# Modulation sums by whole rows, tied in program order, and moved later

## The chip, the cores and the metric

The kernel runs on one core of a Trainium2 chip. The metric is the device time in microseconds. Engines named below: PE (TensorE, matrix multiply), DVE (VectorE), ACT (ScalarE), POOL (GpSimd) and SP (SyncE, whose queue issues most transfers).

## The reference

512 latent tokens and 256 context tokens of width 1024 pass through two blocks of two layers each, in float32. Every layer begins with a modulated norm, whose shift, scale and gate are a vector times a matrix:

```python
shift_x, scale_x, gate_x = jnp.split(jax.nn.silu(c) @ w_mod + b_mod, 3, axis=-1)
hx = rms_norm(xs, norm_g) * (1 + scale_x[:, None]) + shift_x[:, None]
...                                     # block 1: conv, GLA and attention branches
xs = xs + gate_x[:, None] * merge(px, ya_x, yb_x, yc_x)
```

In block 1 the context has its own modulation from `c_ctx` and the same matrix; its second layer updates the latent alone. In block 2 `silu(c_2) @ w_ada` gives shift, scale and gate of each layer; the layers mix with mLSTM heads and retention heads.

## The kernel before

Activations lie as [128 partitions, 8 x tokens]. Every projection is three matmuls of split halves (`mm3`, line 315). A weight pack of 512 KB is loaded on the SP queue (`raw`, line 268), its high part is copied by ACT (line 283), its low part subtracted by DVE (line 284); two raw and two split packs exist at a time.

**Modulation.** Layer 0 of block 1 gets its shift and scale at the start, by matmuls. All other 80 groups of 128 outputs ("rows", one tile of [128, 1024] weights each) are multiplied and summed on DVE: `mod_gen` loads a half row of 512 columns (line 404, SP queue, tag `mw`, four buffers, three loads ahead) and runs a multiply-sum instruction per half row and vector (line 415; the profile shows it as a custom instruction and a read of the accumulator). A first half starts from the bias, a second half from the first's result. Rows for layer 0's gates and for layer 1's shift and scale are summed with two vectors (`c`, `c_ctx`). `conditions` loads the vectors and applies silu, half a row at a time (lines 382 to 389).

**Order of the work.** The program is traced once, layer by layer; generators are woven by hand (`_weave`, `_lifted`). Each `proj_gen` and each piece of `proj_n` ends in a `tick`, which adds `bg_rate` to an account and for every whole unit on it advances the list `K.bg` by a step: a half row, or a vector of `conditions`. `K.bg` is filled ahead of each layer's attention stage: in layer 0 with the conditions, `gate0` and `mod1` at 1.4 a tick, in layer 1 with the third condition, `mod2` and `mod3` at 1.2. `drain` runs what is left of a named list: `gate0` and the next layer's list before the layer's last projection, `mod3` before the end of block 2's first layer.

After tracing, a planner puts each engine's instructions in order: by its own times, of what is ready it takes what was traced first, so an instruction that is ready early can pass others that wait. `_lifted` makes it prefer a generator by 200 places. `tc.keep_in_program_order(ins)` ties an instruction behind the one traced before it on its engine; what comes later isn't tied by it.

**Stages.** Layer 0: start to 65 us; conv taps on DVE (line 806) beside projections; conv norm (lines 820 to 868); four GLA heads (lines 930 to 1025; a reciprocal square root, `rsqrt`, lines 300 to 306, in each head's two segments) woven with the first merge; attention (`kv_in`, `grp_in`, `heads`) woven with `gated` and the second merge; then the gated attention output, the third merge (`merge(ab_, "w_attn_out", 2, done=fin)`) and the output projection. Layer 1 is the same with 512 tokens in the outputs. Block 2 runs from some 1630 us.

Of the kernel before, what the change touches and what calls it, by code (L numbers as in the profile page):

```python
# [9 lines left out]
F32 = mybir.dt.float32  # L10
F32R = mybir.dt.float32r
BF16 = mybir.dt.bfloat16
U8 = mybir.dt.uint8
I32 = mybir.dt.int32
AF = mybir.ActivationFunctionType
ALU = mybir.AluOpType
# [3 lines left out]
P = 128  # L20
D = 1024
# [236 lines left out]
class _K:  # L258
# [33 lines left out]
    def rsqrt(self, x, tag=""):  # L292

        V = self.nc.vector
        n = x.shape[1]
# [81 lines left out]

    def conditions(self, first, n):

        S = self.nc.scalar  # L380
        self.cond = self.cst.tile([P, 2, D], F32, tag="cond", name="cond")
        S.dma_start(out=self.cond[:, :n, :], in_=self.a["cond"][:, first:first + n, :])
        for i in range(n):
            for o in range(0, D, 512):
                c = self.cond[:, i, o:o + 512]
                t = self.mp.tile([P, 512], F32, tag="mw", name="mt")
                S.activation(t, c, AF.Tanh, scale=0.5)
                S.activation(c, c, AF.Copy, scale=0.5)
                self.nc.vector.scalar_tensor_tensor(out=c, in0=t, scalar=1.0, in1=c, op0=ALU.add, op1=ALU.mult)
            yield True  # L390

    def mod_gen(self, idx, todo):


        V = self.nc.vector
        todo = [(j, vecs, o) for j, vecs in todo for o in (0, 1)]
        out, bias = self.mods[idx], self.bmod[idx]
        ws, part = [], {}

        def load(n):  # L400
            if n < len(todo):
                j, _, o = todo[n]
                w = self.mp.tile([P, 512], F32, tag="mw", name="mw")
                self.nc.sync.dma_start(out=w, in_=self.a["modw"][idx, j, :, 512 * o:512 * o + 512])
                ws.append(w)
        for n in range(3):
            load(n)
        for n, (j, vecs, o) in enumerate(todo):
            load(n + 3)
            w = ws.pop(0)  # L410
            for v, b in vecs:
                if o == 0:
                    part[b] = self.mp.tile([P, 1], F32, tag=f"pt{b}", name="pt", bufs=2)
                junk = self.mp.tile([P, 512], BF16, name="junk", bufs=1)
                V.tensor_tensor_reduce(out=junk, in0=w, in1=self.cond[:, v, 512 * o:512 * o + 512], scale=1.0,  # L415
                                       scalar=part[b] if o else bias[:, j:j + 1], op0=ALU.mult, op1=ALU.add,
                                       accum_out=out[:, j, b:b + 1] if o else part[b])
            yield True


# [39 lines left out]
    def hidden(self, x, rstd, i, b, s, e, k, t3):  # L460

        V, S = self.nc.vector, self.nc.scalar
        t = t3()[:, :e - s]
        sh = self.mods[i][:, k, b:b + 1]
        V.scalar_tensor_tensor(out=t, in0=x[:, k, s:e], scalar=self.gsc[:, k, b:b + 1], in1=rstd, op0=ALU.mult,
                               op1=ALU.mult)
        S.activation(self.hh[:, k, s:e], t, AF.Identity, bias=sh)
        V.scalar_tensor_tensor(out=self.hl[:, k, s:e], in0=t, scalar=sh, in1=self.hh[:, k, s:e].bitcast(F32),  # L468
# [104 lines left out]
def _first_block(K, ctx, resp):  # L573
    tc, nc, a = K.tc, K.nc, K.a
    V, S, G, T = nc.vector, nc.scalar, nc.gpsimd, nc.tensor
    ident, ones, eps = K.ident, K.ones, K.eps
# [7 lines left out]
    def layer(l, res, t3p, ctx2, pend):  # L584
# [57 lines left out]
        mod = K.mods[l]  # L642
        first = None
        if l == 0:
            with tc.tile_pool(name="m0", bufs=16) as m0, tc.tile_pool(name="m0ps", bufs=1, space=PSUM) as mq:
# [38 lines left out]
                ws = [mod_in(p_, 0) for p_ in (0, 1)]  # L684
# [361 lines left out]
            _weave(gla, merge(cb, "w_conv_out", 0, True), n_gla - n0, 24 if need else 16)  # L1046


        if l == 0:
            K.bg = [("c", K.conditions(0, 2)),  # L1050
                    ("gate0", K.mod_gen(0, [(j, ((0, 0), (1, 1))) for j in range(16, 24)])),
                    ("mod1", K.mod_gen(1, [(j, ((0, 0), (1, 1)) if j < 16 else ((0, 0),)) for j in range(24)]))]
            K.bg_rate = 1.4
        else:
            K.bg = [("c", K.conditions(2, 1))]
            K.bg += [(f"mod{i}", K.mod_gen(i, [(j, ((0, 0),)) for j in range(24)])) for i in (2, 3)]
            K.bg_rate = 1.2


        with tc.tile_pool(name="att", bufs=1) as ap, tc.tile_pool(name="attps", bufs=1, space=PSUM) as pa:  # L1060
# [185 lines left out]
            def heads(g, ao):  # L1246
                prev = None
                qTs = [head_in(g, 0)]
                for i in range(4):
# [14 lines left out]
            _weave(_chain(heads(0, ao), grp_in(1), heads(1, ao)), _lifted(tc, merge(gb_, "w_gla_out", 1), 200),  # L1264
                   *((114, 32) if need else (72, 16)))

        ab_ = []
        for _ in gated(ao, C_AG, "bag", 0.5, ab_, U, A):
            pass
# [33 lines left out]
        with tc.tile_pool(name="nps", bufs=4, space=PSUM) as nps:  # L1303
            if not need:
                K.new_h()

            K.drain("gate0", f"mod{l + 1}")

            def norm_a():
                if need:  # L1310
                    K.new_h()
                K.gains(l + 1)
                return K.norm_gen(new, accA, l + 1, 0, *A, t3, lambda: nps.tile([P, 512], F32, name="nps"))
            K.out_norm(K.out_gen("w_out", l, 0, mhl, A, B, evac, not need), norm_a)
# [12 lines left out]
def _second_block(K, ctx, res, pend):  # L1327
    tc, nc, a = K.tc, K.nc, K.a
    V, S, G, T = nc.vector, nc.scalar, nc.gpsimd, nc.tensor
# [49 lines left out]
    def last(acc, s, e):  # L1379
        r = []  # L1380
        yield from K.rstd_gen(acc, pb, r)
        for k in range(KT):
# [4 lines left out]
            if k % 2:  # L1387
                yield

    norm_b = pend(tt, pb)  # L1390
    PAIRS = [(i, j) for j in range(4) for i in range(j, 4)]
    PIDX = {p: n for n, p in enumerate(PAIRS)}
# [3 lines left out]
    for l in range(DEPTH):  # L1396
# [8 lines left out]
        mod = K.mods[2 + l].rearrange("p a b -> p (a b)")  # L1405
# [237 lines left out]
        for hd in range(4):  # L1643
            y += mixer("m", hd)
            if l == 0 and hd == 0:
                tables()
        for ob in range(KT):
            evac(ob, *K.proj_t(("w_out_2", l, 0, 8, 128 * ob, 128), y, XS)[0])
        y = []
# [21 lines left out]
def build(tc, a):  # L1671
    nc = tc.nc
    K = _K(tc, a)
    with ExitStack() as ctx:
        cst = K.cst = ctx.enter_context(tc.tile_pool(name="cst", bufs=1))
        K.identr = cst.tile([P, P], F32R, name="identr")
        K.ident = K.identr.bitcast(F32)
        K.ones = cst.tile([P, 8], F32, name="ones")
        nc.gpsimd.memset(K.ones, 1.0)
        K.eps = cst.tile([P, 1], F32, name="eps")  # L1680
        nc.gpsimd.memset(K.eps, EPS)
        K.hpi = cst.tile([P, 1], F32, name="hpi")
        nc.gpsimd.memset(K.hpi, float(np.pi / 2))
        V, S = nc.vector, nc.scalar
        c1_, c2_ = _S1["c"], _S2["c"]
        cv = cst.tile([P, 24], F32, name="cv")
        S.dma_start(out=cv[:, 0:16], in_=a["small1"][0, :, c1_:c1_ + 16])
        S.dma_start(out=cv[:, 16:24], in_=a["small2"][0, :, c2_:c2_ + 8])
        K.bmod = []
        for i, (arr, l, off) in enumerate((("small1", 0, _S1["bmod"]), ("small1", 1, _S1["bmod"]),  # L1690
                                           ("small2", 0, _S2["bada"]), ("small2", 1, _S2["bada"]))):
            t = cst.tile([P, 24], F32, name=f"bmod{i}")
            S.dma_start(out=t, in_=a[arr][l, :, off:off + 24])
            K.bmod.append(t)
        K.ngs = []
        for i, (arr, l, off) in enumerate((("small1", 0, _S1["ng"]), ("small1", 1, _S1["ng"]),
                                           ("small2", 0, _S2["ng"]), ("small2", 1, _S2["ng"]))):
            t = cst.tile([P, 8], F32, name=f"ng{i}")
            S.dma_start(out=t, in_=a[arr][l, :, off:off + 8])
            K.ngs.append(t)  # L1700
        K.mods = [cst.tile([P, 24, 2 if i < 2 else 1], F32, name=f"mod{i}") for i in range(4)]
        ct = cst.tile([P, 24], F32, name="ct")
        S.activation(ct, cv, AF.Tanh, scale=0.5)
        V.tensor_scalar(out=cv, in0=cv, scalar1=0.5, scalar2=None, op0=ALU.mult)
        V.scalar_tensor_tensor(out=ct, in0=ct, scalar=1.0, in1=cv, op0=ALU.add, op1=ALU.mult)
        K.cpad = cst.tile([P, KT, 32], F32, name="cpad")
        nc.gpsimd.memset(K.cpad, 0.0)
        V.tensor_copy(out=K.cpad[:, :, 0:3], in_=ct.rearrange("p (b k) -> p k b", b=3))
        K.selm = cst.tile([P, 3], F32, name="selm")
        S.dma_start(out=K.selm, in_=a["selm"])  # L1710
        K.sp = ctx.enter_context(tc.tile_pool(name="sp", bufs=2))
        K.mp = ctx.enter_context(tc.tile_pool(name="mp", bufs=4))
        K.wr = ctx.enter_context(tc.tile_pool(name="wr", bufs=2))
        K.wh = ctx.enter_context(tc.tile_pool(name="wh", bufs=2))
        K.hp = ctx.enter_context(tc.tile_pool(name="hid", bufs=1))
        eye = K.mp.tile([P, 256], F32, name="accB", bufs=1)
        nc.scalar.dma_start(out=eye[:, :P], in_=a["ident"])
        S.activation(K.identr, eye[:, :P], AF.Copy)
        resp = ctx.enter_context(tc.tile_pool(name="resp", bufs=1))
        with ExitStack() as c1:  # L1720
            x, pend = _first_block(K, c1, resp)
        with ExitStack() as c2:
            _second_block(K, c2, x, pend)
# [20 lines left out]
```

## Time and profile before

| | |
|---|---|
| median of 3 runs | 2816.28 us (2813.78 to 2820.03) |
| profiled execution, its time | 2818.03 us |
| its span | 2816.2 us |
| mean granted PE clock | 0.966 of full speed |
| busy in the span | PE 94%, PEld 81%, DVE 71%, ACT 38%, POOL 1% |
| chain that ended last | PE 79%, DVE 13%, ACT 3%, issue 2%, DMA 2% |
| line 404 (`mw`) transfers | 160 of 256 KB, median 3.1 us to landing |
| line 268 (`wr`) transfers | 308 of 512 KB, 3.6 us; 48 of 256 KB, 2.7 us |

Busy time is what an engine spent in instructions; matmuls are pipelined, so their durations overlap and a busy PE need not be at its peak. The granted clock is the share of full speed that PE was given. The chain is followed back from the last instruction to what released each step. A wait is put down to the event that came last.

### The profile page before, as it was taken

To read this page: it belongs to the slowest core of one execution; us is meant where nothing else is said; L and a number is where in the kernel's file an instruction comes from. 1 tells how busy PE (TensorE), PEld (TensorE's weight loads), DVE (VectorE), ACT (ScalarE), POOL (GpSimd) and SP (SyncE) were. 2 spreads that over 40 slices of the span, in tenths; PEclk is the share of its full clock that TensorE was granted. 3 is DMA by queue.
4 is the path that set the end of the run, shared out by engine and by line. 5 is a ranking of instruction groups with operands and counts; after the bars stand their busy time and mean duration, and the time that the engine had idled before them with its cause. 6 is when DMAs were issued, how large, how long until landed. Compare 5 with 4: busy or idle time off the path is not lost.

```text
span 2816.2 us, 38989 instructions
## 1 busy us (share of the span) xinstructions
PE 2646.8 (94%) x15260; PEld 2290.9 (81%) x15260; DVE 2003.1 (71%) x3912; ACT 1082.4 (38%) x1800; POOL 25.9 (1%) x93
## 2 busy tenths in 40 slices
PE   5897798799999999699999999999999999999998
PEld 4786677788888878577888898888888988888887
DVE  5999988877763489777678477764666687745655
ACT  4243332245552233343456345442333444432332
POOL 0000000000000000000000000000000000000000
PEclk9998898799999999799999999999999999999999
DMA  6221345630111322112211332222232222322322
GB/s 241 77 66 49 113 136 184 201 97 30 42 47 60 109 86 70 34 49 75 74 53 46 98 103 85 83 76 80 81 95 68 83 78 90 90 68 83 93 73 75
DMA packets 89208, 242.26 MB, mean 86 GB/s; under 512 B 11200, under 2 KB 17728, under 8 KB 88768
## 3 DMA queue, kind: packets, MB, share of 16 engines
q1 hardware_dynamic: 83968, 233.38, 27.2%
q10 hardware_dynamic: 5056, 6.39, 0.7%
q8 instruction: 120, 1.97, 0.3%
q14 instruction: 64, 0.52, 0.1%
HBM read 237.64 MB, written 2.10 MB: 85 GB/s over the span
## 4 chain that ended last, share of the span: by engine, by line
PE 79%; DVE 13%; ACT 3%; issue 2%; DMA 2%; DVEq 0%; ACTq 0%
PE pp L315 63%; PE pm L315 5%; PE ov L1236 2%; DVE ca L806 2%; PE sc L1206 2%; PE tr L1226 2%; DVE SP L992 2%; DVE wl L284 1%; DVE junk L415 1%; DMA mw<-modw 1%; ACT wh L283 1%; PE pm L1017 1%; PE pm L621 1%; PE pm L631 1%; PE pm L1013 1%
## 5 line engine op out<-in xcount | busy, mean ns | idle before, releaser
L315 PE MATMUL pp<-hh,wh 128*128 128x512 f32 (+1 forms) x2080 | 774.8, 375 | 21.5 <-ACT wh L283 8.9
L315 PE MATMUL pp<-hh,wl 128*128 128x512 f32 (+1 forms) x2080 | 770.6, 373 | 16.2 <-DVE wl L284 16.2
L315 PE MATMUL pp<-hl,wh 128*128 128x512 f32 (+1 forms) x2080 | 771.0, 372 | 1.5 <-DVE hl L468 1.3
L283 ACT ACTIVATE wh<-wr 128x1024 fp32r<-128x1024 f32 (+1 forms) x316 | 314.1, 995 | 731.4 <-PE pp L315 615.1
L284 DVE TENSOR_TENSOR wl<-wr,wh 128x1024 fp32r<-128x1024 f32 (+1 forms) x316 | 360.2, 1140 | 221.5 <-ACT wh L283 218.7
L315 PEld LDWEIGHTS pp<-hh,wh 128*128 128x128 f32 x2080 | 398.9, 192 | 89.0 <-ACT wh L283 11.1
L315 PEld LDWEIGHTS pp<-hh,wl 128*128 128x128 f32 x2080 | 398.6, 192 | 87.1 <-DVE wl L284 20.8
L315 PEld LDWEIGHTS pp<-hl,wh 128*128 128x128 f32 x2080 | 399.0, 192 | 66.2 <-DVE hl L468 3.4
L806 DVE SCALAR_TENSOR_TENSOR ca<-u,sm,ca 128x783 f32<-128x783 f32 (+1 forms) x240 | 200.8, 886 | 0.4
L315 PE MATMUL pp<-hl,hh 128*128 128x256 f32 x544 | 155.8, 286 | 2.6 <-DVE hl L284 2.5
L315 PE MATMUL pp<-hh 128*128 128x256 f32 x544 | 155.5, 286 | 0.9 <-ACT u L1502 0.9
L315 PE MATMUL pp<-hh,hl 128*128 128x256 f32 x544 | 155.3, 285 | 0.0
L315 PE MATMUL pp<-wl,hh 128*128 128x256 f32 x448 | 128.6, 288 | 1.7 <-DVE wl L284 1.7
L315 PE MATMUL pp<-wh,hh 128*128 128x256 f32 x448 | 126.6, 288 | 3.6 <-ACT tf L736 3.6
L315 PE MATMUL pp<-wh,hl 128*128 128x256 f32 x448 | 127.4, 286 | 0.0
L315 PE MATMUL pp<-bh,wh 128*128 128x512 f32 (+1 forms) x288 | 104.9, 367 | 9.0 <-ACT bh L864 6.6
L315 PEld LDWEIGHTS pp<-hl,hh 128*128 128x128 f32 x544 | 105.7, 194 | 4.1 <-DVE hl L284 3.5
L315 PEld LDWEIGHTS pp<-hh 128*128 128x128 f32 x544 | 105.8, 194 | 3.2 <-ACT u L1502 1.7
L315 PEld LDWEIGHTS pp<-hh,hl 128*128 128x128 f32 x544 | 105.9, 195 | 0.0
L315 PE MATMUL pp<-bh,wl 128*128 128x512 f32 (+1 forms) x288 | 103.3, 360 | 0.7 <-DVE wl L284 0.7
L315 PE MATMUL pp<-bl,wh 128*128 128x512 f32 (+1 forms) x288 | 103.5, 361 | 0.0
L315 PE MATMUL pp<-yh,wh 128*128 128x512 f32 (+1 forms) x256 | 94.5, 369 | 0.0
(372 smaller groups left out, 4930.2 us busy)
## 6 DMA issues: line engine op xcount, KB each, us to landing
wr<-wpack SPq DMA_DIRECT2D x308, 512.0 KB, 3.6
mw<-modw SPq DMA_DIRECT2D x160, 256.0 KB, 3.1
wr<-wpack SPq DMA_DIRECT2D x48, 256.0 KB, 2.7
m<-wpack SPq DMA_DIRECT2D x16, 512.0 KB, 8.9
res<-xT SPq DMA_DIRECT2D x4, 512.0 KB, 5.0
tf<-xT SPq DMA_DIRECT2D x8, 256.0 KB, 2.8
out<-t SPq DMA_DIRECT2D x16, 128.0 KB, 1.8
cond<-cond ACTq DMA_DIRECT2D x1, 1024.0 KB, 8.5
```

Of the source, the lines that this page charges most:

```text
L283: self.nc.scalar.activation(hi, r, AF.Copy)
L284: self.nc.vector.tensor_tensor(out=lo, in0=r, in1=hi.bitcast(F32), op=ALU.subtract)
L315: mm(o, lhsT=lhs[a], rhs=r[b], start=first and p == 0, stop=last and p == 2)
L415: V.tensor_tensor_reduce(out=junk, in0=w, in1=self.cond[:, v, 512 * o:512 * o + 512], scale=1.0, scalar=part[b] if o else bias[:, j:j + 1] ...
L621: T.matmul(p1[:, i:i + 1], lhsT=x[:, o:o + P], rhs=ones[:, 0:1], start=True, stop=True)
L631: T.matmul(p2[:, o:o + P], lhsT=r[:, i:i + 1].to_broadcast([P, P]), rhs=ident, start=True, stop=True)
L806: V.scalar_tensor_tensor(out=ca[:, c, :], in0=x, scalar=w, in1=ca[:, c, :], op0=ALU.mult, op1=ALU.add)
L992: V.scalar_tensor_tensor(out=SP[r, n_, :], in0=SP[r, c_, :], scalar=dec[r, c_:c_ + 1], in1=con[c_][r, :], op0=ALU.mult, op1=ALU.add)
L1013: T.matmul(op[:, p * P:p * P + P], lhsT=gv[:, p0 + p, vh], rhs=asum[:, p * P:p * P + P], start=True, stop=False)
L1206: T.matmul(sc[:, s - k0:e - k0], lhsT=qT[:, t * P:t * P + P], rhs=kT[pi][:, s:e], start=pi == 0, stop=pi == 1)
L1226: T.transpose(tr[:, jj * 256 + q * P:jj * 256 + q * P + P], pr[q][:, (j + jj) * P:(j + jj + 1) * P], ident)
L1236: T.matmul(ov, lhsT=vhl[:, kts[j0 + jj], g].rearrange("p a b -> p (a b)"), rhs=x_[:, jj * 256:jj * 256 + 256], start=j0 + jj + pi == 0, st ...
```

## The change

Whole rows: `mw` tiles hold 1024 columns, in two buffers instead of four, one load ahead instead of three, and one multiply-sum serves a row and vector; the account's unit is a row, and a list's first step is its first load alone. Each multiply-sum, and the Tanh and the last instruction of `conditions`, are tied in program order. The rates and lists are new: 0.3 a tick from the attention stage on, 1.3 from the gated attention output on (under the third merge), 0.5 from block 2 on; layer 0 has the conditions, `gate0` and the 16 rows of layer 1's shift and scale; the other rows are in layer 1's lists, with a drain for `gate2` in block 2.

```diff
     def conditions(self, first, n):
...
-            for o in range(0, D, 512):
...
+            c = self.cond[:, i, :]
+            t = self.mp.tile([P, D], F32, tag="mw", name="mt")
+            pin(S.activation(t, c, AF.Tanh, scale=0.5))
+            S.activation(c, c, AF.Copy, scale=0.5)
+            pin(self.nc.vector.scalar_tensor_tensor(out=c, in0=t, scalar=1.0, in1=c, op0=ALU.add, op1=ALU.mult))
             yield True
     def mod_gen(self, idx, todo):
-        V = self.nc.vector
-        todo = [(j, vecs, o) for j, vecs in todo for o in (0, 1)]
+        V, pin = self.nc.vector, self.tc.keep_in_program_order
...
-                w = self.mp.tile([P, 512], F32, tag="mw", name="mw")
-                self.nc.sync.dma_start(out=w, in_=self.a["modw"][idx, j, :, 512 * o:512 * o + 512])
+                w = self.mp.tile([P, D], F32, tag="mw", name="mw")
+                self.nc.sync.dma_start(out=w, in_=self.a["modw"][idx, todo[n][0]])
                 ws.append(w)
-        for n in range(3):
-            load(n)
-        for n, (j, vecs, o) in enumerate(todo):
-            load(n + 3)
+        load(0)
+        yield True
+        for n, (j, vecs) in enumerate(todo):
+            load(n + 1)
             w = ws.pop(0)
             for v, b in vecs:
...
+                junk = self.mp.tile([P, D], BF16, name="junk", bufs=1)
+                pin(V.tensor_tensor_reduce(out=junk, in0=w, in1=self.cond[:, v, :], scale=1.0,
+                                           scalar=bias[:, j:j + 1], op0=ALU.mult, op1=ALU.add,
+                                           accum_out=out[:, j, b:b + 1]))
             yield True
...
+        c_x, c_ctx = (0, 0), (1, 1)
         if l == 0:
             K.bg = [("c", K.conditions(0, 2)),
-                    ("gate0", K.mod_gen(0, [(j, ((0, 0), (1, 1))) for j in range(16, 24)])),
-                    ("mod1", K.mod_gen(1, [(j, ((0, 0), (1, 1)) if j < 16 else ((0, 0),)) for j in range(24)]))]
-            K.bg_rate = 1.4
+                    ("gate0", K.mod_gen(0, [(j, (c_x, c_ctx)) for j in range(16, 24)])),
+                    ("mod1", K.mod_gen(1, [(j, (c_x, c_ctx)) for j in range(16)]))]
         else:
-            K.bg = [("c", K.conditions(2, 1))]
-            K.bg += [(f"mod{i}", K.mod_gen(i, [(j, ((0, 0),)) for j in range(24)])) for i in (2, 3)]
-            K.bg_rate = 1.2
+            K.bg = [("gate1", K.mod_gen(1, [(j, (c_x,)) for j in range(16, 24)])),
+                    ("c", K.conditions(2, 1)),
+                    ("mod2", K.mod_gen(2, [(j, (c_x,)) for j in range(16)])),
+                    ("gate2", K.mod_gen(2, [(j, (c_x,)) for j in range(16, 24)])),
+                    ("mod3", K.mod_gen(3, [(j, (c_x,)) for j in range(24)]))]
+        K.bg_rate = 0.3
...
+        K.bg_rate = 1.3
         ab_ = []
...
-            K.drain("gate0", f"mod{l + 1}")
+            K.drain("gate0", "mod1", "gate1", "mod2")
...
+    K.bg_rate = 0.5
     norm_b = pend(tt, pb)
...
+        K.drain("gate2")
         for ob in range(KT):
             evac(ob, *K.proj_t(("w_out_2", l, 0, 8, 128 * ob, 128), y, XS)[0])
...
-        K.mp = ctx.enter_context(tc.tile_pool(name="mp", bufs=4))
+        K.mp = ctx.enter_context(tc.tile_pool(name="mp", bufs=2))
```

## Rows read from the trace of the kernel before

**Rows 1.** By stretch: its length; busy PE, PEld, DVE, ACT, POOL; clock; DMA share, GB/s
```profile
65.00:231.00 166.00, 150.95 (x935) 134.05 (x935) 165.67 (x205) 52.44 (x77) 0.00 (x0) 0.96 0.22 65
231.00:285.00 54.00, 43.84 (x232) 38.05 (x233) 49.21 (x111) 19.97 (x26) 0.00 (x0) 0.85 0.22 64
285.00:530.00 245.00, 200.93 (x1180) 175.17 (x1180) 209.55 (x580) 69.27 (x106) 0.00 (x0) 0.84 0.50 158
530.00:600.00 70.00, 61.19 (x373) 55.04 (x373) 59.62 (x135) 25.28 (x40) 0.00 (x0) 0.93 0.53 163
600.00:840.00 240.00, 238.28 (x1523) 207.68 (x1522) 173.50 (x321) 128.44 (x258) 0.00 (x0) 1.00 0.13 40
840.00:932.00 92.00, 92.00 (x530) 81.06 (x529) 35.28 (x45) 26.15 (x38) 0.00 (x0) 1.00 0.22 64
1190.00:1320.00 130.00, 118.63 (x727) 98.77 (x727) 87.26 (x191) 53.85 (x79) 0.00 (x0) 0.99 0.20 59
1320.00:1440.00 120.00, 117.80 (x690) 101.14 (x688) 92.72 (x183) 62.77 (x110) 0.00 (x0) 1.00 0.22 67
...
1545.00:1608.00 63.00, 63.00 (x276) 51.55 (x275) 30.66 (x42) 22.81 (x32) 0.00 (x0) 1.00 0.32 97
1630.00:2010.00 380.00, 375.36 (x2135) 326.83 (x2134) 253.95 (x499) 154.74 (x269) 10.89 (x36) 0.99 0.29 87
```

**Rows 2.** The same by stretch for line 415 alone: DVE busy, clock, DMA
```profile
65.00:231.00 166.00, 11.29 (x30) 0.96 0.22 65
231.00:285.00 54.00, 11.41 (x31) 0.85 0.22 64
285.00:530.00 245.00, 108.89 (x288) 0.84 0.50 158
530.00:600.00 70.00, 25.77 (x68) 0.93 0.53 163
```

**Rows 3.** DVE in order of time, conv norm of layer 0: start, duration, instruction
```profile
247.60 0.17 DVE L637 TENSOR_SCALAR v<-pm 128x6 f32<-128x6 f32 x1 [1.96 <-PE pm L621]
...
249.15 0.75 DVE L415 CUSTOM_DVE_ANT_0 junk<-mw,cond,pt 128x512 bf16<-128x512 f32 x1
...
249.95 0.75 DVE L415 CUSTOM_DVE_ANT_0 junk<-mw,cond,bmod 128x512 bf16<-128x512 f32 x1
...
256.62 0.16 DVE L306 SCALAR_TENSOR_TENSOR y<-t,y 128x6 f32<-128x6 f32 x1
```

**Rows 4.** DVE in order of time, a GLA head of layer 1
```profile
1233.24 0.16 DVE L637 TENSOR_SCALAR v<-pm 128x4 f32<-128x4 f32 x1 [4.78 <-PE pm L621]
...
1235.42 0.16 DVE L306 SCALAR_TENSOR_TENSOR y<-t,y 128x4 f32<-128x4 f32 x1
```

**Rows 5.** Chain that ended last, 231 to 600 us, shares by line
```profile
by line: PE pp L315 33.7%; issue 8.4%; DVE junk L415 7.7%; DMA mw<-modw 6.9%; DVE SP L992 4.8%; PE pm L1017 3.6%; PE pm L621 3.2%; PE pm L1013 2.7%; DVE wl L284 2.2%; PE pm L631 2.0%; DVE at L1005 1.0%; DVE merged L863 1.0%; DVE cd L862 1.0
```

**Rows 6.** What PE waited for, 231 to 600 us: total, times, longest
```profile
PE pm L972 <- DVE bk L966: 14.3, 3, 11.9
PE pm L631 <- DVE y L306: 13.4, 4, 5.7
```

**Rows 7.** PE and ACT in order of time, at the start
```profile
21.08 3.64 PE L664 MATMUL mq<-m,cpad 128*32 128x512 f32 x16
...
24.60 1.15 ACT L387 ACTIVATE mt<-cond 128x512 f32<-128x512 f32 x2 [7.50 <-DMA cond<-cond]
...
26.17 0.57 ACT L667 ACTIVATE t<-mq 128x512 f32<-128x512 f32 x1
```

**Rows 8.** DVE instructions by shape, 231 to 600 us: busy, mean ns, idle before
```profile
L284 DVE TENSOR_TENSOR wl<-wr,wh 128x1024 fp32r<-128x1024 f32 x21 | 25.6, 1220 | 3.2 <-ACT wh L283 3.0
...
L284 DVE TENSOR_TENSOR wl<-wr,wh 128x512 fp32r<-128x512 f32 x9 | 6.2, 687 | 2.5 <-ACT wh L283 2.5
```

**Rows 9.** Transfers issued, whole span: count, KB each, median us to landing
```profile
wr<-wpack SPq DMA_DIRECT2D x308, 512.0 KB, 3.6
```

**Rows 10.** What the sync queue waited for, 231 to 600 us: total, times, longest
```profile
SPq L404 <- DVE pt L415: 53.4, 38, 6.7
```

More of the change, by code (lines that the diff above doesn't have):

```diff
@@ L378, in conditions @@
     def conditions(self, first, n):
-        S = self.nc.scalar
+        S, pin = self.nc.scalar, self.tc.keep_in_program_order
         self.cond = self.cst.tile([P, 2, D], F32, tag="cond", name="cond")
@@ L383, in conditions @@
         for i in range(n):
-            for o in range(0, D, 512):
[L385 to L389, printed above, removed]
+            c = self.cond[:, i, :]
+            t = self.mp.tile([P, D], F32, tag="mw", name="mt")
@@ L390, in conditions @@
+            pin(S.activation(t, c, AF.Tanh, scale=0.5))
+            S.activation(c, c, AF.Copy, scale=0.5)
+            pin(self.nc.vector.scalar_tensor_tensor(out=c, in0=t, scalar=1.0, in1=c, op0=ALU.add, op1=ALU.mult))
             yield True
     def mod_gen(self, idx, todo):
-        V = self.nc.vector
-        todo = [(j, vecs, o) for j, vecs in todo for o in (0, 1)]
+        V, pin = self.nc.vector, self.tc.keep_in_program_order
         out, bias = self.mods[idx], self.bmod[idx]
-        ws, part = [], {}
+        ws = []
@@ L400, in load @@
         def load(n):
             if n < len(todo):
-                j, _, o = todo[n]
-                w = self.mp.tile([P, 512], F32, tag="mw", name="mw")
-                self.nc.sync.dma_start(out=w, in_=self.a["modw"][idx, j, :, 512 * o:512 * o + 512])
+                w = self.mp.tile([P, D], F32, tag="mw", name="mw")
+                self.nc.sync.dma_start(out=w, in_=self.a["modw"][idx, todo[n][0]])
                 ws.append(w)
-        for n in range(3):
-            load(n)
-        for n, (j, vecs, o) in enumerate(todo):
-            load(n + 3)
+        load(0)
@@ L410, in mod_gen @@
+        yield True
+        for n, (j, vecs) in enumerate(todo):
+            load(n + 1)
             w = ws.pop(0)
             for v, b in vecs:
[L412 to L417, printed above, removed]
+                junk = self.mp.tile([P, D], BF16, name="junk", bufs=1)
+                pin(V.tensor_tensor_reduce(out=junk, in0=w, in1=self.cond[:, v, :], scale=1.0,
+                                           scalar=bias[:, j:j + 1], op0=ALU.mult, op1=ALU.add,
+                                           accum_out=out[:, j, b:b + 1]))
```

## The prediction

> **What bounds the kernel now.** I read the page's slices first: TensorE (PE) is at 9 tenths or more from about 650 us on, and short of it before. So the next view was the table of engine time by stretch [rows 1]. From 65 to 600 us, which is layer 0's conv, GLA and the first part of its attention stage, PE idles 15.1 + 10.2 + 44.1 + 8.8 = 78 us and its granted clock is 0.84 to 0.96, that is, part of that time it runs at the lower of its two levels (1.2 instead of 2.4 GHz). From 600 us to the end of the third merge PE is busy for 330 of 332 us at full clock. VectorE (DVE) in turn is busy for 484 of the 535 us before 600.
>
> What is on it there? The same table for line 415, the multiply-sum of the modulation, cut by stretch [rows 2]: 15, 16, 144 and 34 instructions with as many reads of the accumulator, 208 in all, so every one of them, those for block 2 too, runs before 600 us. They are traced in the attention stages, but the planner lets ready work pass what isn't ready, and these are ready early. What that does is seen in the order of time on DVE [rows 3]: the steps of one reciprocal square root of twelve 0.17 us instructions each have a multiply-sum of 0.75 us put in front of them (the next starts 0.80 us later), so that it lasts from 247.60 to 256.78, 9.2 us. The same code in layer 1, where no multiply-sum is left, takes 2.3 us [rows 4]. The chain of waits from 231 to 600 us [rows 5] has 7.7% under line 415, 6.9% under the landing of its weights and part of the 8.4% "issue": 54 us of 369 without the last. The list of waits shows where PE pays directly [rows 6]: 13.4 us for the end of such a root, 14.3 us for `bk`, which is made on the same crowded engine.
>
> **The change, part by part.** The profiled execution took 2818.0 us (span 2816.2, 1.8 us around it), 1.7 us above the median of the runs shown; the sum is made against 2818.0.
>
> Start. The conditions' Tanh is now tied behind ScalarE's earlier work and can't run at 24.6 us, where ScalarE stood 7.5 us for its transfer and then kept the copy of line 667, whose matmuls end at 24.72, until 26.17 [rows 7]. That gives 1.4 us; bounds 0 and 4.
>
> 65 to 231 us (conv taps). DVE is busy for 165.7 of 166 us; 15 multiply-sums at 0.80 us leave, 12 us. PE idles 15 us, so it can follow. I take 10, bounds 0 and 15.
>
> 231 to 285 us (norm after the conv, DVE and PE in turns). 15.5 x 0.80 = 12 us leave DVE, of which 6.9 us in the one root. I take 9, bounds 3 and 12.
>
> 285 to 530 us (four GLA heads woven with the first merge). 144 x 0.80 = 115 us leave a DVE that is busy for 210 of 245. PE's work at full clock lies between busy time less all time lost to the clock, 200.9 - 0.16 x 245 = 162 us, and the same where the idle time took as much of the low clock as it can: the clock 0.84 is 78 us at half speed, 44 of them idle, 34 busy, 17 lost, so 184. The same stage of layer 1, without multiply-sums, has 118.6 us of PE at 0.99 in 130 us, 0.90 of its time. 162 and 184 at 0.90 are 180 and 204 us, so 41 to 65 us are gained. I take 50, in the middle: the heads of layer 0 have a second segment with a root of its own, for which layer 1 has no row.
>
> 530 to 600 us. Work between 61.2 - 0.07 x 70 = 56 and 61 us, at layer 1's 117.8 of 120 us that is 57 to 62: gain 8 to 13, I take 10. The sum of what goes is 80 us, with bounds 52 and 109.
>
> What comes back. The 208 half rows become 104 whole ones. A whole row's price is not in the trace; the subtraction of a weight pack is, in both widths: 687 and 1220 ns [rows 8], 0.53 us for 512 more columns, so 0.75 + 0.53 + 0.08 = 1.36 us, 141 us in all against 208 x 0.80 = 166. Where they go follows from the rates: in layer 0's attention stage 29 ticks (3 for keys and values, 4 gated, 16 of the merge, 6 for queries) at 0.3 are 8 units, the two conditions, the first load and 5 rows of two sums; under the third merge 20 ticks at 1.3 take the other 19 rows, 38 sums. Layer 1: 27 ticks give the load and 7 sums, its third merge about 23, and block 2 the last 26, one in two ticks, up to about 2010 us. All other instructions stay.
>
> Cost of each, by what is free beside it [rows 1], since the trace has none there: below nothing is excluded, as work only comes; at most it is the whole of the sums. Layer 0 attention: 10 x 1.36 = 14 us plus the conditions on a DVE with 66 of 240 us free and a PE that idles 1.7: I take 3 (0 to 16). Third merge of layer 0: its 16 ticks last 92 us, 5.75 us each, of which DVE is busy for 2.2; while the rows last, 1.3 units of 2.7 us a tick add 3.5, so DVE is full for some 15 ticks, but the weights are split one pack ahead: 3 (0 to 52). Layer 1 attention: 1 (0 to 10). Its third merge: 16 ticks bring 20.8 loads of 512 KB, 10.9 MB in 63 us or 173 GB/s beside the 97 that are there, and 28 us on a DVE with 32 free; a pack of 512 KB now lands in 3.6 us [rows 9] and is asked for one pack ahead: 4 (0 to 31). Block 2: 35 us on a DVE with 126 of 380 us free, PE idles 4.6: 4 (0 to 35). Together 15, bounds 0 and 144; the value is near the lower end because the nearest rows (third merge and block 2) show PE 98 to 100% busy with DVE half idle.
>
> The drains find their lists empty: layer 0 has 28 units and 34 turns, layer 1 needs 27 of 34 before its own.
>
> One thing speaks against the two buffers instead of four. On the sync queue the loads of modulation rows stood 53.4 us, 38 times, up to 6.7 us, for the sum that frees their buffer, with the weight packs behind them on the same queue [rows 10]. The Trainium skill, DMA: Bandwidth & Descriptors, section on the anatomy of one DMA, says that a semaphore wait is served on the issuing sequencer before dispatch, so that what is queued behind waits too; the trace agrees, with these 53.4 us. By that rule alone every load tied to a late sum delays weights, and the change would be the first rival below; by the rows the queue is free again as soon as DVE has time, and the sum stands.
>
> 2818.0 - 80 + 15 = 2753 us.
>
> **The rivals.**
> 1. Slower: the sync queue. With two buffers each of the 80 loads waits at its head for a sum two rows back, in merges where DVE is nearly full, and PE waits for the pack behind it. For: [rows 10], and the nearly full DVE. Against: packs are asked for one ahead, and a tick of these merges lasts 63 / 16 = 3.9 to 5.75 us. At the longest wait seen for half rows, 6.7 us, less some 5 us of that cover, 1.7 us per load, 136 us: 2818 - 80 + 136 = 2874 us. It decides from 1 us per load on. Chance 5%.
> 2. Other waits take the place. PE's waits for line 415 are partly hidden by scans, state updates and ScalarE that come just as late. Then only what the chain lists under line 415 outside its transfers goes, 28 us of [rows 5], with 12 of the conv: 2818 - 40 + 15 = 2793 us. Against: layer 1 shows 0.90 with the same scans. 18%.
> 3. DVE becomes the bound under the third merges and in block 2: half of the 38, 23 and 26 sums, 59 us, on the path: 2818 - 80 + 4 + 59 = 2801 us. For: the fill worked out above. Against: PE never waits in these merges now, and sums run in front of nothing but one split. 10%.
> 4. It does not do what it says: the planner puts other ready work (taps, splits) into the gaps of the roots. Layer 1's roots show a gap filled only now and then, 2.3 us. Time then 2805 to 2818. 3%.
>
> **How the numbers follow.** My forecast, 2753 us, has 64%, its own range 2728 to 2775 (gains 62 to 95 less costs of 5 to 20). Rivals 2 and 3 reach to about 2801. The range 2725 to 2800 holds the forecast's case and most of these two, some 85%. Two runs can't be told apart below 0.2%, 5.6 us. Slower by more: rival 1, 5%; within: most of rival 4, 2%; faster: 93%.
>
> **What will show it.** Right: no line 415 before about 530 us; roots of 2 to 3 us in layer 0; the stretch from the conv's last tap to the attention's first scores shorter by 60 to 70 us with a clock above 0.95; third merges and block 2 with PE at 98% or more. Wrong: PE waiting for `wl` or weight transfers around the third merges or in block 2 (rivals 1, 3); the GLA stage as long as now, with PE waiting for `bk`, `SP` or ScalarE (rival 2).

## The result and the profile after

The changed kernel takes 2766.25 us (median of 4 runs, 2765.05 to 2767.35) against 2815.03 us of the kernel before, run beside it: a ratio of 0.9825, 95% interval [0.9808, 0.9842]. The profiled execution took 2766.78 us, 51.3 us less than that of before. Forecast were 2753 us, between 2725 and 2800. The sign came true and the size was 13 us too hopeful; the mechanism held in a wider form than it was told in. One of the ten executions of experiment 4 took 9567 us at a granted clock of 0.44, and no ratio uses it.

First the table by stretch of the changed kernel, columns as in [rows 1], at the stages' new places: conv taps, conv norm, GLA heads with the first merge, start of the attention, third merge, layer 1's third merge, block 2.

```profile
65.00:225.00 160.00, 150.70 (x938) 133.75 (x938) 155.98 (x173) 52.47 (x78) 0.00 (x0) 0.99 0.19 56
225.00:275.00 50.00, 41.34 (x212) 35.30 (x213) 41.40 (x84) 18.83 (x25) 0.00 (x0) 0.77 0.07 22
275.00:467.00 192.00, 178.30 (x1143) 152.25 (x1143) 113.85 (x271) 65.80 (x101) 0.00 (x0) 0.96 0.16 49
467.00:535.00 68.00, 67.27 (x435) 60.65 (x434) 42.11 (x89) 28.33 (x44) 0.00 (x0) 1.00 0.21 66
780.00:880.00 100.00, 100.00 (x576) 88.13 (x575) 71.14 (x104) 29.51 (x41) 0.00 (x0) 1.00 0.49 143
1505.00:1562.00 57.00, 56.93 (x247) 46.03 (x246) 46.78 (x71) 21.25 (x30) 0.00 (x0) 1.00 0.74 238
1580.00:1960.00 380.00, 376.58 (x2146) 328.48 (x2145) 282.30 (x551) 151.84 (x268) 11.82 (x36) 0.99 0.40 120
```

From 275 to 535 us PE idles 14 us in 260, where it idled 53 in 315, and its clock is 0.96 to 1.00 instead of 0.84 to 0.93. The conv norm is the exception, with a clock of 0.77 where it had 0.85, so that from 227 to 535 us the mean is 0.94 (0.84 there before), a little short of the 0.95 that was named as a sign. In the third merges and in block 2 it is as busy as before, beside a DVE and DMA engines that do more. Next, where the sums (now line 410) run. Columns: stretch and its length, DVE time in sums and their reads (in brackets how many of both), clock, DMA share, GB/s.

```profile
275.00:467.00 192.00, 0.00 (x0) 0.96 0.16 49
467.00:535.00 68.00, 0.00 (x0) 1.00 0.21 66
535.00:680.00 145.00, 7.70 (x12) 1.00 0.16 48
680.00:780.00 100.00, 20.56 (x32) 0.95 0.25 72
780.00:880.00 100.00, 33.48 (x52) 1.00 0.49 143
1140.00:1390.00 250.00, 6.42 (x10) 0.99 0.23 68
1390.00:1505.00 115.00, 12.83 (x20) 1.00 0.38 111
1505.00:1562.00 57.00, 19.34 (x30) 1.00 0.74 238
1580.00:1960.00 380.00, 32.01 (x50) 0.99 0.40 120
```

No sum is left before 535 us. The root of the conv norm, which had taken from 247.60 to 256.78 [rows 3], now looks like the one of layer 1 [rows 4]. DVE in order of time:

```profile
244.12 0.17 DVE L632 TENSOR_SCALAR v<-pm 128x6 f32<-128x6 f32 x1 [1.97 <-PE pm L616]
244.20 0.69 DVE L284 TENSOR_TENSOR wl<-wr,wh 128x512 fp32r<-128x512 f32 x1
244.81 0.17 DVE L300 TENSOR_SCALAR g<-v 128x6 int32<-128x6 int32 x1
245.01 0.17 DVE L301 TENSOR_SCALAR g<-g 128x6 int32<-128x6 int32 x1
...
246.82 0.17 DVE L306 SCALAR_TENSOR_TENSOR y<-t,y 128x6 f32<-128x6 f32 x1
```

It is one of eleven between the conv's end and the keys. From the first instruction of line 300 to the last of line 306 they took 85.8 us together before (3.3 to 10.5 each) and take 24.9 (2.1 to 3.2 each): 61 us less, while the stretch as a whole, from the conv norm's first mean to the attention's first scores, became 61.5 us shorter. That the two agree so closely proves nothing by itself; experiment 6 has clean roots and loses time all the same. PE's waits from 225 to 545 us show the other side; the 13.4 us for `y` and 14.3 us for `bk` of [rows 6] are 1.3 and 3.6:

```profile
PE pm L998 <- DVE SP L987: 6.0, 4, 2.1
...
PE pm L967 <- DVE bk L961: 3.6, 2, 1.9
...
PE pm L626 <- DVE y L306: 1.3, 4, 0.7
```

The state update `SP` of the GLA heads is the largest wait now.

### The profile page after: what moved, and what is told of

Same layout as the page of the kernel before. It is cut to its first block, busy times and chain, and to the rows that moved or that the text cites. A ratio compares the mean times of both kernels' runs of the same rounds, so it can differ in the third digit from the quotient of the medians.

```text
span 2764.9 us, 38527 instructions
## 1 busy us (share of the span) xinstructions
PE 2632.3 (95%) x15260; PEld 2272.7 (82%) x15260; DVE 1987.7 (72%) x3701; ACT 1076.3 (39%) x1792; POOL 26.8 (1%) x93
## 4 chain that ended last, share of the span: by engine, by line
PE 78%; DVE 15%; ACT 3%; issue 2%; DMA 2%; SPq 0%; ACTq 0%; DVEq 0%
PE pp L315 63%; PE pm L315 5%; DVE ca L801 4%; PE ov L1234 2%; DVE wl L284 2%; DVE SP L987 2%; PE sc L1204 2%; PE tr L1224 2%; ACT wh L283 1%; PE pm L626 1%; PE pm L616 1%; PE pm L1012 1%; PE pm L1624 1%; DVE t L941 1%; DVE t L939 0%
## 5 line engine op out<-in xcount | busy, mean ns | idle before, releaser
L410 DVE CUSTOM_DVE_ANT_0 junk<-mw,cond,bmod 128x1024 bf16<-128x1024 f32 x104 | 132.8, 1277 | 3.9 <-DMA mw<-modw 3.6
```

Source lines behind the costliest of these rows:

```text
L410: pin(V.tensor_tensor_reduce(out=junk, in0=w, in1=self.cond[:, v, :], scale=1.0, scalar=bias[:, j:j + 1], op0=ALU.mult, op1=ALU.add, accum ...
```

## Experiments

Differences within a few us between single traces are read with care: up to 75 us, where the edits hardly reach, the traces of these kernels already lie up to 6 us apart. "At equal work" below compares two traces at the moment when PE has done the same number of matmul columns. A root is the chain of instructions of one reciprocal square root, a tail the last stretch of an attention stage.

**1. The tie alone.** The kernel before with only the sums tied; old lists, rates, half rows, four buffers.

```diff
-                V.tensor_tensor_reduce(out=junk, in0=w, ...)
+                self.tc.keep_in_program_order(V.tensor_tensor_reduce(out=junk, in0=w, ...))
```

> The kernel before with its half-row sums tied in program order, and nothing else. Theory: no sum before the attention stage of layer 0, first scores at about 535 us as in the changed kernel, most of the gain there, 2765 to 2785 us; the sums, at 1.4 and 1.2 a tick, crowd the attention stages, which costs 5 to 20 us more than the changed kernel's lists. Rival 'lists': without the new lists nothing is gained, 2805 to 2825 us.

Measured: 2767.35 us, ratio 0.9829 [0.9808, 0.9851]. That is the whole gain. Its first sum runs at 465.3 us. Whole rows, two buffers, new lists and rates together add nothing to it that can be measured. By experiment 8 this looks like two effects that cancel: half rows with the new lists come to 2759.55 and 2759.88 us, below this run, and whole rows give that back. The two kernels were not run beside each other.

**2. All but the tie.** The changed kernel with the sums untied; its conditions stay tied.

```diff
-                pin(V.tensor_tensor_reduce(out=junk, in0=w, ...))
+                V.tensor_tensor_reduce(out=junk, in0=w, ...)
```

> The changed kernel with its sums not tied (whole rows, new lists and rates stay). Theory (the planner lets ready sums pass waiting work, and the tie alone stops that): the sums are back before 600 us, between the steps of the roots, time 2800 to 2818 us. Rival 'load' (what helps is that the lists hand the sums out later and more slowly): the sums stay in the attention stages and merges, 2760 to 2775 us.

Measured: 2782.32 us, 0.9882 [0.9862, 0.9902]: 16 us of the gain go, not 34 to 52; the time lies between the two theories. The sums did not go back to the GLA stage. The tied last instruction of `conditions`, which every sum of layer 0 reads, ran at 464.7 us, so no sum could run ahead of that; the first ran at 490.3. From there on they do what they did before: in the attention stage (10.5 us from 653.7 on) and in block 2's first norm a root has sums in it again. DVE in order of time, that norm:

```profile
1604.22 0.16 DVE L300 TENSOR_SCALAR g<-nv 128x2 int32<-128x2 int32 x1
1604.29 1.28 DVE L410 CUSTOM_DVE_ANT_0 junk<-mw,cond,bmod 128x1024 bf16<-128x1024 f32 x1
...
1608.10 1.27 DVE L410 CUSTOM_DVE_ANT_0 junk<-mw,cond,bmod 128x1024 bf16<-128x1024 f32 x1
...
1613.36 0.15 DVE L306 SCALAR_TENSOR_TENSOR y<-t,y 128x2 f32<-128x2 f32 x1
```

9.3 us, against 5.4 with the tie; PE waited 4.3 us for its end. At equal work this kernel is even with the changed one at 1500 us and some 15 us behind at 1665.

**3. No sums at all.** The changed kernel without conditions, loads and sums.

```diff
-            load(n + 1)
-            ...
-                pin(V.tensor_tensor_reduce(out=junk, in0=w, ...))
+        for _ in range(len(todo) + 1):
             yield True
```

> The changed kernel without conditions, modulation loads and sums (all modulation but layer 0's shift and scale is left out and set to a constant). What the sums still cost where they are now. Theory (they cost about 11 us in layer 0's attention tail, 3 to 6 in layer 1's, nothing in block 2): 2745 to 2753 us. Rival (the costs of the prediction hold, merges and block 2 pay as well): 2735 to 2745. If the start's 1.4 us exists at all, first hidden columns come 1 to 2 us earlier here.

Measured: 2756.16 us, 0.9792 [0.9776, 0.9809]. This lies above both theories, and it is the floor: in the kernel before all sums together cost 2813.86 - 2756.16 = 58 us, and 80 us were never to be had. In the changed kernel they cost about 10. At equal work the kernel without sums is 67 us ahead of the kernel before at 600 us, and 61 ahead at its end: 4 of the difference are lost between 1250 and 1340 us, in layer 1, where neither kernel has a sum left. The cause of that was not sought, and no row of the kernel before shows it.

**4. Without the loads.** The kernel before, every sum reading one tile that is loaded once (the products of the other rows are left out). The pool's four buffers, which only the conditions use then, are three.

```diff
-                w = self.mp.tile([P, 512], F32, tag="mw", name="mw")
-                self.nc.sync.dma_start(out=w, in_=self.a["modw"][idx, j, :, 512 * o:512 * o + 512])
-                ws.append(w)
+                if self.mwfix is None: ...      # one tile, one load
+                ws.append(self.mwfix)
```

> The kernel before with all sums reading one tile that is loaded once (the products of other rows are left out, the sums stay, untied). Theory (the sums' place on VectorE costs, the sync queue and the landings little): roots still 8 to 11 us long, 2795 to 2815 us, the difference to before being the 25 us that the chain books on landings, at most. Rival 'queue' (loads at the head of the sync queue and late landings were the cause): 2760 to 2775 us.

Measured: 2817.24 us (median of nine), 1.0017 [1.0005, 1.0029]: nothing gained by 42 MB fewer transfers, and rival 'queue' is out. Nothing holds the sums for their data now, and they crowd more: 126 instead of 110 us of them between 275 and 535 us. What PE waited for from 225 to 600 us:

```profile
PE pm L633 <- DVE y L307: 18.7, 4, 9.0
PE pm L974 <- DVE bk L968: 15.1, 3, 11.9
PE pm L1015 <- DVE t L1011: 11.1, 4, 7.2
```

So the transfers listed in the chain [rows 5, `mw<-modw` 6.9%] can go without any time going with them, as long as the sums stay where they are on DVE. As the sums also moved together here, a small cost of the loads is not excluded.

**5. Short sums.** The kernel before, each sum over 8 of its 512 columns (the other columns are left out), same count, same loads.

```diff
-                V.tensor_tensor_reduce(out=junk, in0=w, in1=self.cond[:, v, 512 * o:512 * o + 512], ...)
+                V.tensor_tensor_reduce(out=junk[:, :8], in0=w[:, :8], in1=self.cond[:, v, 512 * o:512 * o + 8], ...)
```

> The kernel before with each sum over 8 columns instead of 512 (the rest of each product is left out; loads, lists, order rules and instruction count stay). Theory (each sum's length in a dependent chain costs): a sum of about 0.2 us, roots of 3 to 5 us, 2760 to 2780 us. Rival 'queue': the loads are the same and wait as before, so 2795 us and more.

Measured: 2768.78 us, 0.9846 [0.983, 0.9861]. It is DVE's time in the sums that costs, not their number: 208 instructions in the same stages, 48 instead of 157 us of DVE, and 45 us of the 58 are back; the roots take 2.1 to 5.1 us. The rest, 17 us against experiment 3 at equal work, is lost by 595 us, with DVE still giving 48 us to sums there and all loads (179 GB/s from 275 to 467 us) squeezed in beside the weights; these two were not told apart. That loads have a part in it is likely: ahead of these short sums DVE stood 29.5 us, 39 times, for the landing of a load (9.7 us, 12 times, in the kernel before), and PE once waited 5.3 us for such a sum.

**6. Tied, but early.** The changed kernel with layer 0's list filled before the first merge, at 1.6 a tick.

```diff
+            if l == 0:
+                K.bg = [("c", ...), ("gate0", ...), ("mod1", ...)]
+                K.bg_rate = 1.6
             _weave(gla, merge(cb, "w_conv_out", 0, True), ...)
```

> The changed kernel with layer 0's list (2 conditions, 24 rows, 48 sums, 64 us of VectorE) filled before the first merge at 1.6 a tick, so that the tied sums run beside the GLA heads. Theory (order, not load): VectorE has 78 of 192 us free there, the roots stay at 2 to 4 us, the stage grows by 0 to 12 us and layer 0's attention and third merge give back about 11: 2755 to 2768 us. Rival 'load' (VectorE time in that stage is what cost; 115 us of sums cost some 57 us): 64 us of sums cost 25 to 35 us, less 11 given back, 2780 to 2792 us.

Measured: 2776.36 us, 0.9866 [0.9848, 0.9884], between the two theories. The 48 sums run between 311 and 535 us, the roots stay clean (2.1 to 4.1 us), yet 24 us are lost there against experiment 3 at equal work. PE's waits from 225 to 545 us say where:

```profile
PE pp L315 <- DVE merged L762: 13.3, 2, 11.3
PE pm L1008 <- DVE t L1004: 5.4, 4, 2.9
PE pm L998 <- DVE SP L987: 4.1, 4, 2.1
```

The root is only the worst place. The largest is `merged`, in the first merge, which is no root at all. 48 x 1.36 = 65 us of sums cost 24, or 0.37 per us. In the kernel before, with many sums inside the roots, 157 us had cost 66 by 600 us at equal work, or 0.42. So the root is where the loss is seen best, and not most of what makes it: in this stage PE waits for many short DVE steps in turn, and DVE time put among them costs, inside a root or outside. Half of the 24 us comes back against the changed kernel, since nothing is left for the attention's tail.

**7. The high rate later.** The changed kernel with 1.3 a tick from behind the gated output on.

```diff
-        K.bg_rate = 1.3
         ab_ = []
         for _ in gated(ao, C_AG, "bag", 0.5, ab_, U, A):
             pass
+        K.bg_rate = 1.3
```

> The changed kernel with the rate 1.3 set behind the gated attention output instead of ahead of it. Theory (sums traced with the gated output's projections run in the tail of the attention, because those projections do not wait for it, and crowd the last heads on VectorE): fewer than 3 sums in the last 30 us ahead of the gated output, that stretch 6 to 11 us shorter, layer 1 gains 0 to 4: 2752 to 2762 us. Rival (the loss is the whole stage's, by the 0.3 a tick): 2763 to 2768 us.

Measured: 2764.86 us, 0.9827 [0.9809, 0.9845], no difference from the changed kernel, and the rival's range. At equal work with experiment 3, layer 0's tail loses 5 us instead of 11, but the end of layer 1's attention, from 1400 to 1493 us, loses 6 instead of 3, and the span ends 2 us behind the changed kernel's. In layer 0's tail PE still waits 1.8 us for `ao` and 1.4 us for `wl`, with one sum of 1.28 us close ahead of the two instead of three.

**8. Half rows again.** The changed kernel with 512 columns a sum, four buffers, two loads ahead; tie, lists and rates as changed, the conditions in halves too, a unit still a row. Run twice, the second time beside the changed kernel on the same chip.

```diff
+        todo = [(j, vecs, o) for j, vecs in todo for o in (0, 1)]
...
-                w = self.mp.tile([P, D], F32, tag="mw", name="mw")
+                w = self.mp.tile([P, 512], F32, tag="mw", name="mw")
...
-        K.mp = ctx.enter_context(tc.tile_pool(name="mp", bufs=2))
+        K.mp = ctx.enter_context(tc.tile_pool(name="mp", bufs=4))
```

> The changed kernel with half rows again (208 sums, four buffers, two loads ahead), all else as changed. Theory (whole rows are worth their 25 us of VectorE time only where it is full): in the tail of layer 0's attention and under the third merges VectorE is nearly full, 0 to 8 us slower, 2765 to 2775 us. Rival (whole rows are most of the gain): 2785 us or more.

> The half-row run again, beside the changed kernel on the same chip, since three rounds left it open whether it is faster. Theory: whole rows stand in front of a weight split for 1.28 us where half rows stand for 0.75, so half rows are 4 to 7 us faster: 2757 to 2762 us. Rival: the difference was scatter, and both are within 2 us of each other, at 2761 to 2766 us.

> The changed kernel itself, unedited, as the other side of that comparison. Theory: 2764 to 2768 us, 4 to 7 us above the half rows. Rival: within 2 us of them.

Measured: 2759.55 us, 0.9815 [0.98, 0.9831]; then 2759.88 us (2756.54 to 2763.70), 0.9801 [0.9777, 0.9826], with the changed kernel at 2770.51 us (2762.99 to 2770.99), 0.983 [0.9805, 0.9855]. Half rows are faster, 7 and 11 us by the medians, though sums and reads keep DVE busy for 157 us instead of 134; the first theory had them slower. The size is not known well: side by side the runs of each kernel spread over 7 to 8 us, and the ratios to the kernel before differ by only 3 and 8 us. Buffers and loads ahead changed with the length of a sum and were not tested by themselves. What the length does is seen at the end of layer 0's attention. The changed kernel by stretch, then the half rows:

```profile
745.00:755.00 10.00, 6.08 (x41) 4.79 (x39) 9.51 (x20) 6.30 (x14) 0.00 (x0) 0.95 0.33 95
755.00:765.00 10.00, 7.84 (x20) 5.83 (x21) 9.87 (x13) 1.64 (x3) 0.00 (x0) 0.53 0.53 168
```

```profile
745.00:755.00 10.00, 9.96 (x68) 9.02 (x67) 9.43 (x24) 5.87 (x13) 0.00 (x0) 1.00 0.18 54
755.00:765.00 10.00, 10.00 (x57) 8.55 (x56) 10.00 (x20) 5.58 (x9) 0.00 (x0) 1.00 0.41 131
```

DVE is full in both. In the changed kernel it reaches what PE needs too late; DVE, then PE, in order of time:

```profile
751.04 1.27 DVE L410 CUSTOM_DVE_ANT_0 junk<-mw,cond,bmod 128x1024 bf16<-128x1024 f32 x1
...
752.35 0.42 DVE L1242 TENSOR_TENSOR ao<-ov,bt 64x256 f32<-64x256 f32 x1
...
753.68 1.28 DVE L410 CUSTOM_DVE_ANT_0 junk<-mw,cond,bmod 128x1024 bf16<-128x1024 f32 x1
...
755.45 1.28 DVE L410 CUSTOM_DVE_ANT_0 junk<-mw,cond,bmod 128x1024 bf16<-128x1024 f32 x1
...
757.53 1.22 DVE L284 TENSOR_TENSOR wl<-wr,wh 128x1024 fp32r<-128x1024 f32 x1
```

```profile
752.83 0.39 PE L1234 MATMUL ov<-ph,vhl 128*128 128x256 f32 x1 [2.12 <-DVE ao L1242]
...
755.47 0.58 PE L315 MATMUL pp<-hh,wh 128*128 128x256 f32 x1 [1.91 <-ACT tf L731]
...
758.80 0.80 PE L315 MATMUL pp<-hh,wl 128*128 128x512 f32 x1 [1.68 <-DVE wl L284]
759.40 0.63 PE L315 MATMUL pp<-hh,wh 128*128 128x512 f32 x1
```

In the half-row kernel `ao` waits for one sum of 0.75 us there, `wl` is done at 757.0 us, and PE stands for nothing from 750 to 830 us.

**9. Half rows without the tie.** As 8, sums untied, conditions tied.

```diff
-                pin(V.tensor_tensor_reduce(out=junk, in0=w, ...))
+                V.tensor_tensor_reduce(out=junk, in0=w, ...)
```

> The changed kernel with half rows (four buffers, two loads ahead, as in the half-row run) and its sums untied. Untied whole rows at the new lists and rates had come to 2782 us, with no sum before 467 us: something other than the tie held them. Theory: it is the rate. At 0.3 a tick the sums are traced later, and the planner reaches no further ahead for half rows than for whole ones: no sum before about 460 us, 2770 to 2785 us. Rival: two buffers of whole rows held them, since each load waits for a sum two rows back; then four buffers let the half rows slip into the GLA stage before 460 us again, and the time is 2790 to 2815 us.

Measured: 2768.22 us (2765.01 to 2779.52), 0.9835 [0.9806, 0.9864]. The time is below both theories. No sum runs before 467 us, so the two buffers do not hold them. But the test does not show that the rate does: here too the condition's tied instruction ran at 464.4 us and the first sum at 490.9, as in 2. A kernel with the new rate and no tie anywhere was not tried.

**10. Half rows, evenly.** As 8, at 0.6 a tick in the attention stages and 0.8 under the third merges.

```diff
-        K.bg_rate = 0.3
+        K.bg_rate = 0.6
...
-        K.bg_rate = 1.3
+        K.bg_rate = 0.8
```

> The half-row run with its rates evened out: 0.6 a tick in the attention stages instead of 0.3, 0.8 under the third merges instead of 1.3. Theory: what the sums still cost (some 3 us over the run without any, 2756 us) comes where they fill DVE at the tails of the attention stages; spread out they cost no more: 2756 to 2760 us. Rival: in an attention stage, as in GLA, DVE stands in a chain of dependent steps, and each us of sums put there costs 0.35 us of time: some 9 rows more, about 29 us of DVE in both layers together, so 2765 to 2772 us.

Measured: 2773.27 us (2771.50 to 2776.63), 0.9847 [0.9824, 0.9871], 13 us worse: the rival's side, a little above it. At equal work 5 us more are lost in layer 0's tail and 10 at the start of layer 1's attention, where the keys' chain of norm and rotation lies on DVE and PE stood once for it, with the clock at 0.50 after it:

```profile
PE tr L1168 <- ACT t L1158: 8.5, 1, 8.5
```

```profile
1280.00:1290.00 10.00, 6.70 (x31) 6.68 (x32) 5.51 (x10) 3.22 (x6) 0.00 (x0) 0.50 0.33 105
```

Only two sums, 1.5 us, stood in that chain; the planner had also put parts of the GLA's gated output in it. Why it did so is open, and so it is in part luck that the rival's number came out.

## Why the prediction was right, and where it wasn't

The table goes by marks, instructions that both traces have. First the kernel before, with first and last start of each (first scores' maximum; output of the third merge):

```profile
L1209 DVE TENSOR_REDUCE st<-sc x80: 414/949/959, 600.5 to 1534.5; 128x1 f32<-128x768 f32 x64, 128x1 f32<-128x256 f32 x16
L1278 ACT ACTIVATE m<-merged x14: 632/742/853, 854.0 to 1603.2; 128x768 fp32r<-128x768 f32 x7, 128x512 fp32r<-128x512 f32 x7
```

Then the changed kernel (the same two, with the gated attention output between them):

```profile
L1207 DVE TENSOR_REDUCE st<-sc x80: 409/947/959, 534.8 to 1491.2; 128x1 f32<-128x768 f32 x64, 128x1 f32<-128x256 f32 x16
```

```profile
L734 DVE SCALAR_TENSOR_TENSOR ao<-ao,tf x8: 675/820/960, 752.8 to 1502.3; 128x768 f32<-128x768 f32 x4, 128x512 f32<-128x512 f32 x4
```

```profile
L1277 ACT ACTIVATE m<-merged x14: 614/742/855, 801.6 to 1557.2; 128x768 fp32r<-128x768 f32 x7, 128x512 fp32r<-128x512 f32 x7
```

| step | predicted | measured, and by what |
|---|---|---|
| start | -1.4 | 0: the Tanh still runs early, below |
| conv taps | -10 | -4.2, first mean of the norm 231.2 to 227.0 |
| norm | -9 | -6.2, from there to the first GLA output: 52.8 to 46.6 |
| GLA and first attention | -60 | -55.3, from there to the first scores: 316.5 to 261.2 |
| layer 0, attention and third merge | +6 | +13.3, up to the merge's first output, 854.0 to 801.6 |
| layer 1, the same | +5 | +6.4, from there to layer 1's last output, 1603.2 to 1557.2 |
| block 2 | +4 | -5.3, to the end of the span |
| sum | -65 | -51.3 |

The split of the last rows depends on the marks. At equal work layer 0 loses 12 us from 600 to 930 us of the kernel before, layer 1 loses 5, of which experiment 3 loses 4 without any sum, and block 2 gives 1.5 back. The miss lies in what was to go: conv taps 5.8 us, GLA and first attention 4.7, norm 2.8, start 1.4.

**Right: the mechanism, in a wider form.** DVE time of the sums in the stages ahead of the attention is what the 58 us were: gone with the tie (1), there without loads (4), three quarters of it gone with short sums (5). The prediction told it by the links of a root [rows 3]; experiment 6 shows that sums beside clean roots cost nearly as much per us. Rival 2, that scans and state updates would come just as late, holds for little: `SP` and `bk` now are 9.6 us of PE's waits. Rival 4 is out, the roots are clean.

**Mis-sized: conv taps.** 12 us were to leave a DVE that was busy for 165.7 of 166 us [rows 1], and PE to follow by 10; 4.2 came. In the changed kernel DVE is idle for 4 of 160 us there, in experiment 3 as well (156.07 busy). What it waited for from 65 to 290 us says that most of this is two low halves that stand for ACT's copy, both ahead of 72 us:

```profile
DVE wl L284 <- ACT wh L283: 3.0, 2, 1.6
```

Sums had filled that wait before, so their going gave nothing there. Further, each sum overlaps its neighbours: the traces have 9 us of DVE in this stretch that were the sums' alone, not 12. The step that failed is the price: a busy share near 1 was taken for work that PE waits for.

**Failed: the start.** The tie binds an instruction to the one traced before it on its engine, and what is traced before the Tanh on ACT is the issue of the condition's own transfer, which is tied to nothing. ACT in order of time:

```profile
25.01 1.06 ACT L386 ACTIVATE mt<-cond 128x1024 f32<-128x1024 f32 x1 [7.90 <-DMA cond<-cond]
```

It stands as long as before [rows 7]. Only the conditions' last instruction, tied on DVE, moved. It cost nothing to be wrong: the start did not get shorter without the modulation either (3).

**The costs came to the sum, not to the places.** That they add up to 14.4 us against 15 is luck. Layer 0's attention was priced 3 us for a DVE with 66 us free, third merge 3. The merge cost nothing: from its first to its last output it took 2 us less than before. The attention's end cost all, as the traces of 8 show: there softmax, gated output and the next weight split make PE's chain pass through DVE in short steps. The prediction put 10 sums ahead of the third merge's rate and counted the gated output's own ticks as the merge's; in the trace 14 sums run ahead of the gated output at 752.8 us, six of them in its last 17 us, and three sums of 1.28 us put PE 6 us behind. This is rival 3 in one small place; under the merges, which rival 3 named, DVE could be full (in the half-row kernel 9.9 of 10 us from 785 to 795 us, PE 10.0) at no cost. Block 2 gave a little time back; the kernel without sums does not show this there, and its cause was not sought.

**Rival 1, the sync queue.** The hold came, the cost did not. From 500 to 800 us SP stood longer for sums than it had from 231 to 600 us before [rows 10],

```profile
SPq L401 <- DVE mod L410: 77.0, 12, 21.4
```

and four such loads held the queue's head for 17.5 us from 739.6 on. The Trainium skill, DMA: Bandwidth & Descriptors, section on the anatomy of one DMA, says that a semaphore wait is served on the issuing sequencer before dispatch; the trace agrees, with these 77.0 us. PE did not pay: its longest wait for `wl` there is the 1.68 us above, and DVE, not a transfer, was late. Packs are asked for one ahead, as the prediction said.

The price of a whole row, estimated 1.36 us from [rows 8], was 1.28 us and a read of 0.08 that partly overlaps it; the gains of norm and GLA stage lay within their bounds.

## What to carry to other kernels

When an engine that isn't the bound carries filler work, look at it in order of time inside the stages where the bound engine waits for it: there 1 us of filler cost some 0.4 us in the two kernels that price it (66 us of time for 157, 24 for 65), under merges without such a chain next to nothing (157 us of half-row sums, most of them under third merges and in block 2, cost 3.5 by the medians). Read a busy share near 1 with care: some of the work that fills an engine fills waits. Hold filler back by an instruction that really comes late, put it where no dependent chain crosses its engine, and keep its pieces short: 0.75 us instead of 1.28 was worth some 7 to 11 us although it made more work, with buffers changed along with it. Merging pieces to save fixed costs did not pay here, where the length of a piece and not the sum of the work was the limit.

## What the runs showed of the hardware

In these traces idle time of PE was paid a second time in its clock. In the changed kernel PE stood for 2.1, 1.9 and 1.7 us between 750 and 759 us, and from 755 to 765 us its granted clock was 0.53, that is, nearly all of that stretch at the lower of its two levels. Matmuls of 512 columns start 0.43 us apart there until 764 us and 0.23 us after it, so some 7 us of work took about 3 us longer than at the higher level; with the 6 us of waits that is most of the 11 us that layer 0's tail lost at equal work. The half-row kernel had no such waits there, and its clock was 1.00.
